# A transformer block's passage from attention to the MLP: fp32 copies of the first half, subtractions on VectorE, new places in memory

## The chip, the core and the metric

The kernel runs on one core of a Trainium2 chip. The time is device microseconds of one execution; the time before is the median of three runs. The profile is that of one further execution, and its span runs from the first to the last instruction. TensorE (PE, with its weight loads PEld), VectorE (DVE), ScalarE (ACT) and GpSimd (POOL) run side by side, SyncE (SP) issues most DMAs, and each engine takes its instructions in a fixed order.

## The reference

The block takes 1024 tokens of width 1024 through two attention branches and an MLP with squared ReLU. All is fp32. Cut to what the change touches:

```python
mixed = jnp.concatenate([rms_norm(oa, g_out_a[l]), rms_norm(ob, g_out_b[l])], axis=-1)
h_res = h_res + mixed @ w_out[l]
h = rms_norm(h_res, norm_mlp[l])
h_res = h_res + jnp.square(jax.nn.relu(h @ w_up[l])) @ w_down[l]
return rms_norm(h_res, norm_final)
```

Inside `ob`, three branches are gated and added: `out = gb0 * o_cmp + gb1 * o_sel + gb2 * o_win`.

## The kernel before, in words

**Precision.** Each fp32 operand of a large product is split in a high part (ScalarE copies it to fp32r) and a low part (VectorE or GpSimd subtracts the high part): `split`, lines 92 to 99, with lines 94, 95 for plain sources and 97, 98 for scaled ones from PSUM. A product is three matmuls: high by high, high by low, low by high.

**Attention.** The 8 token tiles of 128 rows are worked off in the order 5, 7, 6, 4, 3, 2, 1, 0. `b_done` (lines 851 to 860) ends a branch of a tile: it scales the output by its denominators and gates (line 857) and adds it to what was there (858), on GpSimd. Behind the second branch comes `finalize`. The output projection of a tile stands in `pieces`: one step transposes and splits the tile (700, 701), two steps multiply a column block each (709 to 711) and add it to the residual (713); the last also takes the row's norm (718 to 722) and scales the row by it (212, 214). After the last tile a few pieces are left, and the code of the transition pops them (line 1179).

**Transition.** The MLP's input must be transposed, scaled by the gain and split. Tiles 4 to 7 are the first half H0, tiles 0 to 3 the second, H1. A first-half step `h2_first(k)` transposes one block of 128 columns of four tiles into a PSUM bank of the kind T (there are two) and splits it into B11 (k below 4) or B21; the 8 steps are spread among the remaining pieces. The MLP's first product is made as a Strassen-Winograd scheme of 2 by 2 blocks with 7 products: 1, 2 and 3 take B11, B21, B22, and 4 to 7 take T4, T1, T2, T3, which are sums. `h2_second(j)` (lines 1154 to 1171) makes these for j from 0 to 3: with b the scaled blocks, T1 = b12 - b11, T2 = b22 - T1, T3 = b22 - b12, T4 = T2 - b21. As b11 and b21 exist only as split pairs, two subtractions take the place of one (1160 and 1161, 1167 and 1168). A ScalarE copy of b12 (1159) serves T3. GpSimd makes the first subtraction of T4 and the low parts of T3 and T1, VectorE those of T2 and T4. Product matmuls (`prod`, 1059 to 1065) of a j follow as soon as its blocks are there. The raw sums lie in two buffers under the tag dn, which the W_down blocks need afterwards.

**MLP loop.** For each of 16 groups g of 256 hidden columns, `up(g)` (1075 to 1111) makes the 7 products, adds them to four blocks c11, c21, c22, c12, and `c_done` squares them (1071), and splits them on ScalarE (1072) and GpSimd (1073). Group 0 is done in the transition. `down(g, t)` (1113 to 1127) multiplies them by W_down for 8 tiles, two column blocks each: a down group is 6 matmuls (1124 to 1126) into a bank of kind S and an addition to the residual on VectorE (1127). PSUM has in this stage 3 banks S, 2 T, 1 F and 2 O; a bank is given out in turn among its kind and must have been emptied. Products 1 and 6 are in T, 4 and 7 in O, 2 in F, 5 and 3 in S; 2 down groups follow in S's turn, and so on. Line 1095 empties product 2, 1106 and 1107 product 5, 1110 product 3. Each group's W_up and W_down blocks come by DMA from SP (1012, 1050) and are split (94, 95).

**Memory and order.** Pools are stacked from the left and from the right. When all attention pools on the right are closed, new ones begin at the right end, where cs2 was (gates, denominators), then vp (value tiles), wk and atp (softmax tiles, transposed ones), then the key tiles and the others. A new tile waits for the last readers of the old tiles that it lies over. Right pools of the MLP before: first h2p (all high parts B11 to T4, then all low ones), then mr (W_up blocks cA, cB, r2, r3 and split weights wa, wb). A list scheduler orders each engine's instructions at build time, by program order among those it takes to be ready; products can so be pulled ahead of their place. Product 2 of the next group often is.

Of the kernel before, what the change touches and what calls it, by code (L numbers as in the profile page):

```python
# [10 lines left out]
F32R = mybir.dt.float32r  # L11
BF = mybir.dt.bfloat16
FH = mybir.dt.float16
AF = mybir.ActivationFunctionType
# [42 lines left out]
def build(tc, A, out):  # L57
# [11 lines left out]
    def f32(ap):  # L69
        return ap.bitcast(F32)  # L70

    def mkpool(name, bufs=1, side="left", space=None):
        kw = dict(name=name, bufs=bufs, side=side, reuse_waits="tile")
        if space is not None:
            kw["space"] = space
            kw.pop("side")
        cm = tc.tile_pool(**kw)
        p = cm.__enter__()
        opened.append(cm)

        def close():
            opened.remove(cm)
            cm.__exit__(None, None, None)

        return p, close
# [6 lines left out]
    def split(hi, lo, src, scale=None, eng="A"):  # L92
        if scale is None:
            a = act.activation(hi, src, AF.Copy) if eng == "A" else dve.tensor_copy(hi, src)
            d = dve.tensor_sub(lo, src, f32(hi))  # L95
        else:
            a = act.activation(hi, src, AF.Copy, scale=scale)
            d = dve.scalar_tensor_tensor(lo, src, scale, f32(hi), op0=OP.mult, op1=OP.subtract)
        return a, d
# [247 lines left out]
    def bank(tag, shape, bufs=None):  # L347
        if tag == "F" and nbank[pst["second"]]["F"] == 0:
            tag = "O"
        n = nbank[pst["second"]][tag]  # L350
        p = pst["pool"] if tag in "OF" else psp
        t = p.tile([128, 512], F32, name=tag, tag=tag, bufs=n)
        if len(shape) == 3:
            return t[:, :shape[1] * shape[2]].rearrange("p (a b) -> p a b", a=shape[1])
        return t[:, :shape[1]]
# [495 lines left out]
    def b_done(i, br):  # L851
        o = OT[i, br]
        d = DEN[i, br] = cs2.tile([128, 8], F32, name="den", bufs=4)
        dve.tensor_scalar(d, o[:, :, 64], vsc[:, 2 + br:3 + br], None, op0=OP.mult)
        dve.reciprocal(d, d)
        pool.tensor_mul(d, d, gate[:, i].rearrange("p (h b) -> p b h", b=3)[:, 1 + br])
        pool.tensor_mul(o[:, :, 0:64], o[:, :, 0:64], d[:, :, None].to_broadcast([128, 8, 64]))
        pool.tensor_add(OC[i] if br else OB[i], o[:, :, 0:64], OC[i])
        if br == 0:
            finalize(i)  # L860

# [127 lines left out]

    cs2_close()  # L990
    NP = DFF // 256
    h2p, h2_close = mkpool("h2p", side="right")
    mr, mr_close = mkpool("mr", side="right")
    XN = ("B11", "B21", "B22", "T1", "T2", "T3", "T4")
    XH, XL = ({x: h2p.tile([128, 4, 512], F32R, name=x + y) for x in XN} for y in "hl")
    XOF = {1: "B11", 2: "B21", 3: "B22", 4: "T4", 5: "T1", 6: "T2", 7: "T3"}
    sso = cst.tile([128, NT, 4], F32, name="sso")
    e2 = cst.tile([128, NT], F32, name="e2")
# [6 lines left out]
    def small(tag, dt=F32, name=None):  # L1005
        p = mr if tag in ("cA", "cB", "r2", "r3") else ml[0]
        return p.tile([128, 512], dt, name=name or tag, tag=tag, bufs=1)

    def w_load(g, blk, tag):
        if g < NP:  # L1010
            t = RW[g, blk] = small(tag)
            sp.dma_start(t, A["w_up"][g, blk])

    def w_split(g, n, slot, src):
        if g < NP:
            t = (mr if slot in "ab" else ml[0]).tile([128, 2, 4, 128], F32R, name="w" + slot, tag="w" + slot, bufs=1)
            W[g, n] = t
            s = src.rearrange("p (k c) -> p k c", k=4)
            split(t[:, 0], t[:, 1], s)

    def w_prep(g, first=False):
        if g >= NP:
            return []
        A11, A12, A21, A22 = (RW[g, b] for b in range(4))

        def s1():
            if not first:
                w_split(g, 1, "a", A11)
            w_split(g, 4, "d" if first else "b", A22)

        def s2():
            dve.tensor_sub(A11, A11, A21)
            dve.tensor_add(A21, A21, A22)
            dve.tensor_sub(A22, A22, A11)
            w_split(g, 6, "c", A22)

        def s3():
            if not first:
                w_split(g, 2, "d", A12)
            dve.tensor_sub(A12, A12, A22)  # L1040

        def s4():
            w_split(g, 7, "e", A11)

        return [s1, s2, s3, s4]
# [13 lines left out]
    def prod(g, n, ps, ks=range(4)):  # L1059
        x, w = XOF[n], W[g, n]  # L1060
        for k in ks:
            xh, xl = XH[x][:, k], XL[x][:, k]
            pe.matmul(ps, w[:, 0, k], xh, start=k == 0, stop=False)  # L1063
            pe.matmul(ps, w[:, 0, k], xl, start=False, stop=False)  # L1064
            pe.matmul(ps, w[:, 1, k], xh, start=False, stop=k == 3)  # L1065
# [7 lines left out]
        pool.tensor_sub(lo, a, f32(hi))  # L1073

    def up(g):
        y = {n: bank(x, [128, 512], 2) for n, x in ((1, "T"), (4, "O"), (6, "T"), (2, "F"), (7, "O"), (5, "S"), (3, "S"))}
        for q in range(2):
            d_load(g, q)
        prod(g, 1, y[1])
        c11 = small("u0", name="c11")  # L1080
        act.activation(c11, y[1], AF.Copy)  # L1081
        w_split(g, 5, "a", RW[g, 2])
        for q in range(2):
            d_split(g, q)
        for q in range(2, 4):
            d_load(g, q)
        prod(g, 4, y[4])
        prod(g, 6, y[6])
        c12 = small("cA", name="c12")
        dve.tensor_add(c12, y[6], c11)  # L1090
        w_split(g, 3, "b", RW[g, 1])
        w_load(g + 1, 2, "r2")
        w_load(g + 1, 1, "r3")
        prod(g, 2, y[2])
        dve.tensor_add(c11, y[2], c11)
        c_done(g, 0, 0, c11)
        prod(g, 7, y[7])
        c22 = small("cB", name="c22")
        dve.tensor_add(c22, y[7], c12)
        c21 = small("u1", name="c21")  # L1100
        dve.scalar_tensor_tensor(c21, y[4], -1.0, c22, op0=OP.mult, op1=OP.add)
        c_done(g, 1, 0, c21)
        for q in range(2, 4):
            d_split(g, q)
        prod(g, 5, y[5])
        dve.tensor_add(c22, y[5], c22)
        dve.tensor_add(c12, y[5], c12)
        c_done(g, 1, 1, c22)
        prod(g, 3, y[3])
        dve.tensor_add(c12, y[3], c12)  # L1110
        c_done(g, 0, 1, c12)
# [34 lines left out]
    def h2_ps(h, k):  # L1146
        ps = transposes([hr(h * 4 + t)[:, k * 128:(k + 1) * 128] for t in range(4)])
        return ps.rearrange("p a b -> p (a b)")

    def h2_first(k):  # L1150
        x = "B11" if k < 4 else "B21"
        split(XH[x][:, k % 4], XL[x][:, k % 4], h2_ps(H0, k), scale=gm32[:, k:k + 1])

    def h2_second(j):
        raw = ml[0].tile([128, 4, 512], F32, name="wdx", tag="dn", bufs=2)
        T1, T2, T3, T4 = (raw[:, n] for n in range(4))
        ps = h2_ps(H1, j)
        g = gm32[:, j:j + 1]
        act.activation(T3, ps, AF.Copy, scale=g)
        dve.scalar_tensor_tensor(T1, ps, g, f32(XH["B11"][:, j]), op0=OP.mult, op1=OP.subtract)  # L1160
        dve.tensor_sub(T1, T1, f32(XL["B11"][:, j]))
        ps = h2_ps(H1, j + 4)
        g = gm32[:, j + 4:j + 5]
        dve.scalar_tensor_tensor(T2, ps, g, T1, op0=OP.mult, op1=OP.subtract)
        dve.scalar_tensor_tensor(T3, ps, g, T3, op0=OP.mult, op1=OP.subtract)
        split(XH["B22"][:, j], XL["B22"][:, j], ps, scale=g)
        pool.tensor_sub(T4, T2, f32(XH["B21"][:, j]))
        dve.tensor_sub(T4, T4, f32(XL["B21"][:, j]))
        for x, t, e in (("T2", T2, dve), ("T3", T3, pool), ("T4", T4, dve), ("T1", T1, pool)):
            act.activation(XH[x][:, j], t, AF.Copy)  # L1170
            e.tensor_sub(XL[x][:, j], t, f32(XH[x][:, j]))

    for blk, tag in enumerate(("cA", "r3", "r2", "cB")):
        w_load(0, blk, tag)
    w_split(0, 1, "a", RW[0, 0])
    w_split(0, 2, "b", RW[0, 1])
    rest = len(pieces)
    for n in range(rest):
        pieces.pop(0)[3]()
        for k in range(n * KD // rest, (n + 1) * KD // rest):  # L1180
            h2_first(k)
    wop_close()
    ml[0], ml_close = mkpool("mlq")
    y = {1: bank("F", [128, 512]), 2: bank("O", [128, 512]), 6: bank("O", [128, 512])}
    prod(0, 1, y[1])
    prod(0, 2, y[2])
    for f in w_prep(0, True):
        f()
    w_split(0, 5, "a", RW[0, 2])
# [12 lines left out]
    for j in range(5):  # L1202
        if j < 4:
            h2_second(j)
        if j:
            for n in (6, 7, 4) if j > 2 else (6, 7, 4, 3, 5):
                prod(0, n, y[n], ks=(j - 1,))
# [111 lines left out]
```

## Time and profile before

| | |
|---|---|
| median of 3 runs | 1414.26 us (1410.06 to 1418.48) |
| profiled execution | 1414.72 us, its span 1412.9 us, granted TensorE clock 0.98 |
| busy: PE, PEld | 1313.4 us (93%), 1110.6 us (79%) |
| busy: DVE, ACT, POOL | 970.4 (69%), 650.3 (46%), 512.0 us (36%) |

In a row of a timeline stand the start, the duration, the engine, the line of the kernel, the operation, the tile written and the one read, and in brackets how long the engine had been idle and what ended that. Neighbouring instructions of an engine overlap by a little, so the distance of two starts is the price of one in a row of many. A row of stages has for each engine the busy time and the number of instructions, in the order PE, PEld, DVE, ACT, POOL. A clock of 1.00 is 2.4 GHz.

### The profile page before, as it was taken

The numbers are of one execution on the slowest core, as the hardware profiler recorded it, in microseconds if no ns is written. First come the engines' busy times: TensorE is split into PE (matmuls) and PEld (weight loads), VectorE is DVE, ScalarE is ACT, GpSimd is POOL, SyncE is SP. The second block draws the span as 40 slices with busy tenths as digits, with TensorE's granted clock in tenths as the row PEclk, the third lists the DMA queues.
The fourth block names the chain that finished last, engine by engine and source line by source line (L and its number), as shares of the span: only waits on it lengthen the run. The fifth ranks groups of instructions, "written<-read, shape, count | busy, mean of one in ns | idle before, by whom it ended". The sixth has DMA issues, their size and how long they took to land.

```text
span 1412.9 us, 23742 instructions
## 1 busy us (share of the span) xinstructions
PE 1313.4 (93%) x8891; PEld 1110.6 (79%) x8891; DVE 970.4 (69%) x1953; ACT 650.3 (46%) x1212; POOL 512.0 (36%) x724
## 2 busy tenths in 40 slices
PE   7999999998987999899778999999999999999996
PEld 6788989888976777677656888888888888788885
DVE  6664565773458876878587667677767667776767
ACT  7462755872557866898553222222222212222216
POOL 3445473664445665577542110011111001111115
PEclk9999999999898999999999999999999999999998
DMA  6265382985538986686311121112111111111113
GB/s 189 68 113 120 87 185 51 206 184 145 93 107 180 172 152 129 143 157 96 82 30 34 56 59 46 45 46 60 45 60 46 59 41 50 55 50 61 45 46 134
DMA packets 265747, 131.68 MB, mean 93 GB/s; under 512 B 220064, under 2 KB 240544, under 8 KB 265632
## 3 DMA queue, kind: packets, MB, share of 16 engines
q1 hardware_dynamic: 265488, 129.90, 40.0%
q8 instruction: 70, 1.15, 0.3%
q14 instruction: 45, 0.37, 0.1%
q10 hardware_dynamic: 144, 0.26, 0.0%
HBM read 68.26 MB, written 8.39 MB: 54 GB/s over the span
## 4 chain that ended last, share of the span: by engine, by line
PE 57%; DVE 16%; DMA 8%; issue 7%; POOL 6%; ACT 5%; SPq 1%; DVEq 0%; POOLq 0%; ACTq 0%
PE S L1124 8%; PE S L1125 7%; PE S L1126 7%; PE F L335 3%; PE F L336 3%; PE F L337 3%; DMA u<-in_w_down_dram 3%; PE O L1064 2%; PE O L1063 2%; PE T L1065 2%; PE T L1063 2%; PE T L1064 2%; PE O L1065 2%; PE S L418 2%; DVE c L1071 1%
## 5 line engine op out<-in xcount | busy, mean ns | idle before, releaser
L1073 POOL TENSOR_TENSOR ul<-c,uh 128x512 fp32r<-128x512 f32 x64 | 92.5, 1454 | 557.8 <-ACT uh L1072 555.9
L1127 DVE SCALAR_TENSOR_TENSOR st<-S,r,st 128x512 f32<-128x512 f32 (+1 forms) x257 | 185.8, 742 | 70.3 <-PE S L1126 69.7
L1124 PE MATMUL S<-dn,uh 128*128 128x512 f32 (+1 forms) x514 | 203.2, 396 | 9.6 <-DVE c L1110 5.9
L1126 PE MATMUL S<-dn,ul 128*128 128x512 f32 (+1 forms) x514 | 200.6, 391 | 0.8 <-POOL ul L1073 0.8
L1125 PE MATMUL S<-dn,uh 128*128 128x512 f32 (+1 forms) x514 | 200.8, 391 | 0.0
L335 PE MATMUL F<-wh,hh 128*128 128x256 f32 (+1 forms) x576 | 167.2, 292 | 6.1 <-DVE st L214 3.2
L336 PE MATMUL F<-wl,hh 128*128 128x256 f32 (+1 forms) x576 | 166.5, 289 | 2.3 <-DVE wl L95 2.3
L337 PE MATMUL F<-wh,hl 128*128 128x256 f32 (+1 forms) x576 | 165.4, 288 | 0.0
L1124 PEld LDWEIGHTS S<-dn,uh 128*128 128x128 f32 x514 | 97.2, 189 | 37.8 <-DVE c L1110 12.2
L434 ACT ACTIVATE ns<-ns,mn 128x640 f32<-128x640 f32 (+7 forms) x152 | 110.7, 747 | 35.1 <-POOL mn L433 21.7
L335 PEld LDWEIGHTS F<-wh,hh 128*128 128x128 f32 x576 | 110.7, 193 | 8.2 <-DVE st L214 3.6
L450 POOL TENSOR_TENSOR hl<-ns,hl 128x640 f16<-128x640 f32 (+5 forms) x67 | 105.5, 1575 | 30.9 <-ACT hl L448 24.9
L1126 PEld LDWEIGHTS S<-dn,ul 128*128 128x128 f32 x514 | 97.0, 189 | 22.0 <-POOL ul L1073 1.5
L336 PEld LDWEIGHTS F<-wl,hh 128*128 128x128 f32 x576 | 111.3, 193 | 3.7 <-DVE wl L95 3.1
L1125 PEld LDWEIGHTS S<-dn,uh 128*128 128x128 f32 x514 | 97.4, 190 | 19.2
L337 PEld LDWEIGHTS F<-wh,hl 128*128 128x128 f32 x576 | 111.0, 193 | 0.5
L448 ACT ACTIVATE hl<-ns 128x640 f16<-128x640 f32 (+5 forms) x115 | 91.2, 802 | 5.8 <-DMA pt<-hl 5.0
L468 PE MATMUL O<-v,pt 128*128 128x65 f16 x694 | 77.3, 195 | 15.9 <-DMA pt<-hl 13.4
L1081 ACT ACTIVATE c<-T 128x512 f32<-128x512 f32 x15 | 9.0, 599 | 172.2 <-PE S L1125 172.2
L468 PEld LDWEIGHTS <-pt 128*128 128x128 f16 x694 | 63.9, 99 | 27.6 <-DMA pt<-hl 17.4
L418 PE MATMUL S<-kb,qb 128*128 128x384 f32 (+3 forms) x192 | 72.9, 385 | 12.6 <-DVE mn L429 8.9
L433 POOL TENSOR_SCALAR mn<-mn 128x1 f32<-128x1 f32 x130 | 43.7, 336 | 96.4 <-DVE mn L429 81.2
(372 smaller groups left out, 3625.1 us busy)
## 6 DMA issues: line engine op xcount, KB each, us to landing
u<-in_w_down_dram SPq DMA_DIRECT2D x64, 256.0 KB, 2.8
wr<-in_w_in_dram SPq DMA_DIRECT2D x44, 256.0 KB, 2.9
r<-in_w_up_dram SPq DMA_DIRECT2D x32, 256.0 KB, 2.7
st<-in_x_dram SPq DMA_DIRECT2D x8, 512.0 KB, 5.9
wor<-in_w_out_dram SPq DMA_DIRECT2D x16, 256.0 KB, 3.5
cA<-in_w_up_dram SPq DMA_DIRECT2D x16, 256.0 KB, 2.8
cB<-in_w_up_dram SPq DMA_DIRECT2D x16, 256.0 KB, 2.6
ns<-in_xT_dram SPq DMA_DIRECT2D x7, 512.0 KB, 5.1
```

The source lines that it names most:

```text
L335: pe.matmul(ps, hh[:, k, ts], hi, start=k == 0, stop=False)
L336: pe.matmul(ps, hh[:, k, ts], lo, start=False, stop=False)
L337: pe.matmul(ps, hl[:, k, ts], hi, start=False, stop=k == KD - 1)
L418: pe.matmul(ps[:, :w], u["q"], u["k"][:, cs], start=True, stop=False)
L434: u["exp"] = act.activation(ns[:, :n * 128], ns[:, :n * 128], AF.Exp, scale=-1.0, bias=mn[:, j:j + 1])
L450: pool.tensor_sub(lo, p, hi)
L468: pe.matmul(ps, ph, v[:, 64:129], start=t == 0, stop=False)
L1073: pool.tensor_sub(lo, a, f32(hi))
L1124: pe.matmul(ps, uh[:, ts], wd[:, 0, cs], start=j == 0, stop=False)
L1125: pe.matmul(ps, uh[:, ts], wd[:, 1, cs], start=False, stop=False)
L1126: pe.matmul(ps, ul[:, ts], wd[:, 0, cs], start=False, stop=j == 1)
L1127: dve.scalar_tensor_tensor(o[:, cs], ps, r2[:, t:t + 1], o[:, cs], op0=OP.mult, op1=OP.add)
```

## The change

In `b_done` the last two instructions go to VectorE for the last tile's second branch. The right side of memory is laid out anew: T4's high part first, then mr, then the other block tiles in pairs. In `up`, product 2 gets an S bank and product 3 the F bank. Four first-half steps come before the first weight splits and the remaining pieces, four stay among these. A second transposition of the first half, `h2_again(j)`, puts blocks j and j + 4 into fp32 tiles RB by ScalarE; they lie in the tiles v0 to v3, which the high and low parts of c11 and c21 use later. `h2_second` subtracts RB in place of split pairs; it has no GpSimd instruction and no ScalarE copy of b12 left.

```diff
@@ -854,8 +854,9 @@
         dve.tensor_scalar(d, o[:, :, 64], vsc[:, 2 + br:3 + br], None, op0=OP.mult)
         dve.reciprocal(d, d)
         pool.tensor_mul(d, d, gate[:, i].rearrange("p (h b) -> p b h", b=3)[:, 1 + br])
-        pool.tensor_mul(o[:, :, 0:64], o[:, :, 0:64], d[:, :, None].to_broadcast([128, 8, 64]))
-        pool.tensor_add(OC[i] if br else OB[i], o[:, :, 0:64], OC[i])
+        e = dve if i == ORD[-1] and br == 0 else pool
+        e.tensor_mul(o[:, :, 0:64], o[:, :, 0:64], d[:, :, None].to_broadcast([128, 8, 64]))
+        e.tensor_add(OC[i] if br else OB[i], o[:, :, 0:64], OC[i])
         if br == 0:
             finalize(i)
 
@@ -989,10 +990,15 @@
 
     cs2_close()
     NP = DFF // 256
+    XH, XL = {}, {}
+    h0p, h0_close = mkpool("h0p", side="right")
+    XH["T4"] = h0p.tile([128, 4, 512], F32R, name="T4h")
+    mr, mr_close = mkpool("mr", side="right")
     h2p, h2_close = mkpool("h2p", side="right")
-    mr, mr_close = mkpool("mr", side="right")
-    XN = ("B11", "B21", "B22", "T1", "T2", "T3", "T4")
-    XH, XL = ({x: h2p.tile([128, 4, 512], F32R, name=x + y) for x in XN} for y in "hl")
+    for x in ("B11", "B21", "B22", "T1", "T2", "T3", "T4"):
+        for y, X in (("h", XH), ("l", XL)):
+            if x not in X:
+                X[x] = h2p.tile([128, 4, 512], F32R, name=x + y)
     XOF = {1: "B11", 2: "B21", 3: "B22", 4: "T4", 5: "T1", 6: "T2", 7: "T3"}
     sso = cst.tile([128, NT, 4], F32, name="sso")
     e2 = cst.tile([128, NT], F32, name="e2")
@@ -1073,7 +1079,7 @@
         pool.tensor_sub(lo, a, f32(hi))
 
     def up(g):
-        y = {n: bank(x, [128, 512], 2) for n, x in ((1, "T"), (4, "O"), (6, "T"), (2, "F"), (7, "O"), (5, "S"), (3, "S"))}
+        y = {n: bank(x, [128, 512], 2) for n, x in ((1, "T"), (4, "O"), (6, "T"), (2, "S"), (7, "O"), (5, "S"), (3, "F"))}
         for q in range(2):
             d_load(g, q)
         prod(g, 1, y[1])
@@ -1151,39 +1157,45 @@
         x = "B11" if k < 4 else "B21"
         split(XH[x][:, k % 4], XL[x][:, k % 4], h2_ps(H0, k), scale=gm32[:, k:k + 1])
 
+    RB = {}
+
+    def h2_again(j):
+        for n, k in enumerate((j, j + 4)):
+            t = RB[k] = small("v%d" % (2 * (j % 2) + n), name="b%d1" % (n + 1))
+            act.activation(t, h2_ps(H0, k), AF.Copy, scale=gm32[:, k:k + 1])
+
     def h2_second(j):
         raw = ml[0].tile([128, 4, 512], F32, name="wdx", tag="dn", bufs=2)
         T1, T2, T3, T4 = (raw[:, n] for n in range(4))
         ps = h2_ps(H1, j)
-        g = gm32[:, j:j + 1]
-        act.activation(T3, ps, AF.Copy, scale=g)
-        dve.scalar_tensor_tensor(T1, ps, g, f32(XH["B11"][:, j]), op0=OP.mult, op1=OP.subtract)
-        dve.tensor_sub(T1, T1, f32(XL["B11"][:, j]))
+        dve.scalar_tensor_tensor(T1, ps, gm32[:, j:j + 1], RB[j], op0=OP.mult, op1=OP.subtract)
         ps = h2_ps(H1, j + 4)
         g = gm32[:, j + 4:j + 5]
         dve.scalar_tensor_tensor(T2, ps, g, T1, op0=OP.mult, op1=OP.subtract)
-        dve.scalar_tensor_tensor(T3, ps, g, T3, op0=OP.mult, op1=OP.subtract)
         split(XH["B22"][:, j], XL["B22"][:, j], ps, scale=g)
-        pool.tensor_sub(T4, T2, f32(XH["B21"][:, j]))
-        dve.tensor_sub(T4, T4, f32(XL["B21"][:, j]))
-        for x, t, e in (("T2", T2, dve), ("T3", T3, pool), ("T4", T4, dve), ("T1", T1, pool)):
-            act.activation(XH[x][:, j], t, AF.Copy)
-            e.tensor_sub(XL[x][:, j], t, f32(XH[x][:, j]))
+        dve.tensor_sub(T3, T2, RB[j])
+        dve.tensor_sub(T4, T2, RB[j + 4])
+        for x, t in (("T2", T2), ("T3", T3), ("T4", T4), ("T1", T1)):
+            split(XH[x][:, j], XL[x][:, j], t)
 
     for blk, tag in enumerate(("cA", "r3", "r2", "cB")):
         w_load(0, blk, tag)
+    rest = len(pieces)
+    for k in range(4):
+        h2_first(k)
     w_split(0, 1, "a", RW[0, 0])
     w_split(0, 2, "b", RW[0, 1])
-    rest = len(pieces)
     for n in range(rest):
         pieces.pop(0)[3]()
-        for k in range(n * KD // rest, (n + 1) * KD // rest):
+        for k in range(4 + n * 4 // rest, 4 + (n + 1) * 4 // rest):
             h2_first(k)
     wop_close()
     ml[0], ml_close = mkpool("mlq")
     y = {1: bank("F", [128, 512]), 2: bank("O", [128, 512]), 6: bank("O", [128, 512])}
     prod(0, 1, y[1])
     prod(0, 2, y[2])
+    for j in range(2):
+        h2_again(j)
     for f in w_prep(0, True):
         f()
     w_split(0, 5, "a", RW[0, 2])
@@ -1202,6 +1214,8 @@
     for j in range(5):
         if j < 4:
             h2_second(j)
+        if j < 2:
+            h2_again(j + 2)
         if j:
             for n in (6, 7, 4) if j > 2 else (6, 7, 4, 3, 5):
                 prod(0, n, y[n], ks=(j - 1,))
```

## Rows read from the trace of the kernel before

**Rows 1.** the slices of the span, TensorE.

```profile
PE   7999999998987999899778999999999999999996
```

**Rows 2.** stages: us, busy us (x) of each engine, clock, DMA share, GB/s.

```profile
690.50:698.30 7.80, 3.60 (x24) 2.64 (x24) 2.88 (x6) 2.88 (x9) 3.29 (x5) 1.00 0.50 151
698.30:718.30 20.00, 18.57 (x92) 14.73 (x92) 15.45 (x28) 13.06 (x25) 1.10 (x2) 0.91 0.14 41
718.30:749.70 31.40, 21.52 (x85) 13.75 (x85) 30.65 (x39) 16.15 (x27) 19.55 (x13) 0.95 0.05 18
```

**Rows 3.** timeline of GpSimd, last attention output: start us, us, what.

```profile
695.58 1.04 POOL L857 TENSOR_TENSOR ot<-ot,den 128x512 f32<-128x512 f32 x1
...
697.10 1.19 POOL L858 TENSOR_TENSOR ob<-ot,oc 128x512 f32<-128x512 f32 x1
```

**Rows 4.** timeline of TensorE from the last attention product to the second half.

```profile
693.89 0.20 PE L468 MATMUL O<-v,ptx 128*128 128x65 f16 x1
...
698.33 0.85 PE L360 MATMUL T<-c_ident,ob 128*128 128x128 f32 x4 [4.09 <-POOL ob L858]
...
700.89 1.05 PE L360 MATMUL T<-c_ident,st 128*128 128x128 f32 x4
...
708.23 1.03 PE L360 MATMUL T<-c_ident,st 128*128 128x128 f32 x8
```

**Rows 5.** timeline of VectorE, the second half's beginning.

```profile
718.30 0.74 DVE L1160 SCALAR_TENSOR_TENSOR wdx<-T,gm,B11h 128x512 f32<-128x512 f32 x1
...
719.56 0.69 DVE L95 TENSOR_TENSOR wb<-r,wb 128x512 fp32r<-128x512 f32 x1
720.16 0.68 DVE L1161 TENSOR_TENSOR wdx<-wdx,B11l 128x512 f32<-128x512 f32 x1
...
723.69 1.76 DVE L1161 TENSOR_TENSOR wdx<-wdx,B11l 128x512 f32<-128x512 f32 x1
```

**Rows 6.** instructions by line, 718.3 to 749.7: busy us, mean ns, idle before.

```profile
L1171 DVE TENSOR_TENSOR T2l<-wdx,T2h 128x512 fp32r<-128x512 f32 x4 | 5.1, 1266 | 0.0
...
L1168 DVE TENSOR_TENSOR wdx<-wdx,B21l 128x512 f32<-128x512 f32 x4 | 4.6, 1158 | 0.5 <-POOL wdx L1167 0.5
...
L1161 DVE TENSOR_TENSOR wdx<-wdx,B11l 128x512 f32<-128x512 f32 x4 | 3.8, 953 | 0.0
...
L1171 DVE TENSOR_TENSOR T4l<-wdx,T4h 128x512 fp32r<-128x512 f32 x4 | 3.8, 939 | 0.0
...
L1164 DVE SCALAR_TENSOR_TENSOR wdx<-T,gm,wdx 128x512 f32<-128x512 f32 x4 | 3.0, 744 | 0.1
...
L1170 ACT ACTIVATE T2h<-wdx 128x512 fp32r<-128x512 f32 x4 | 2.5, 631 | 0.9 <-DVE wdx L1164 0.9
```

**Rows 7.** timeline of GpSimd beside it.

```profile
723.18 1.72 POOL L1167 TENSOR_TENSOR wdx<-wdx,B21h 128x512 f32<-128x512 f32 x1
```

**Rows 8.** timeline of TensorE, the start of a later group's down products.

```profile
1044.26 0.39 PE L1063 MATMUL F<-B21h,wd 128*128 128x512 f32 x1
...
1046.76 0.39 PE L1124 MATMUL S<-dn,uh 128*128 128x512 f32 x1
...
1049.20 0.50 PE L1124 MATMUL S<-dn,uh 128*128 128x512 f32 x1 [0.47 <-DVE c L1110]
```

**Rows 9.** timeline of VectorE in the same stretch.

```profile
1042.33 0.69 DVE L95 TENSOR_TENSOR dn<-u,dn 128x512 fp32r<-128x512 f32 x1 [0.60 <-ACT dn L94]
...
1050.87 2.06 DVE L1127 SCALAR_TENSOR_TENSOR st<-S,r,st 128x512 f32<-128x512 f32 x3
```

**Rows 10.** the page's group of line 1124, then product 2 by tile B21h.

```profile
L1124 PE MATMUL S<-dn,uh 128*128 128x512 f32 (+1 forms) x514 | 203.2, 396 | 9.6 <-DVE c L1110 5.9
...
L1063 PE MATMUL F<-B21h,wd x60: 389/389/389, 757.4 to 1337.4; 128*128 128x512 f32 x60
```

**Rows 11.** stages: a middle iteration, the last one's start.

```profile
1005.00:1046.60 41.60, 41.23 (x182) 33.66 (x182) 28.98 (x43) 9.66 (x18) 5.28 (x4) 1.00 0.16 51
1371.00:1385.00 14.00, 11.89 (x43) 8.54 (x42) 12.48 (x18) 5.81 (x11) 4.72 (x4) 0.88 0.34 112
```

## The prediction, made before the changed kernel was run

> **What bounds the kernel now.** I read the slices of the span first: in slices 25 to 39 TensorE is at 9 tenths or more throughout [rows 1]. The loop over the 16 MLP groups is therefore bound by TensorE, and an edit there pays only where TensorE waits. Then I cut the transition into stages [rows 2]. From 690.5 to 698.3 no engine is busy for half of the time: the last attention outputs are awaited. From 698.3 to 718.3 TensorE shows 18.57 us of 20, in part with short transposes at a granted clock of 0.91. From 718.3 to 749.7 VectorE is busy for 30.65 of 31.4 us, while TensorE has only 85 matmuls. So the second half of the transposition is bound by VectorE, and what comes before it by a chain of several engines.
>
> **Part 1, the last attention output on VectorE.** GpSimd starts the multiplication at 695.58, does something else for half a microsecond, and ends the addition at 698.29; TensorE's wait of 4.09 us ends there [rows 3, 4]. That is 2.7 us. On VectorE I take 0.60 us an instruction, the distance between two neighbouring starts there (719.56 and 720.16) for two SBUF inputs [rows 5]. Two make 1.2 to 1.3 us, a gain of 1.4. No row shows this broadcast multiplication on VectorE; with 0.75 us each and one other instruction ahead the gain is 0.5, with nothing lost in between it is 1.5. What is late next is the output projection itself.
>
> **Part 2, four first-half steps earlier.** Each step is 4 transposes, one ScalarE copy, one VectorE subtraction of 0.75 us. Four of them now run among the last projection: four transposes that take 1.05 us, as long as eight do at 708.23, stand in its midst at 700.89 [rows 4]; the slow ones come right behind the wait. After the change they can run in the hole from 690.5 to 698.3, where VectorE is busy 2.88 of 7.8 us [rows 2]. Their tiles no longer lie over the gate table and denominators that the last output reads, but over softmax tiles, read last by the transposing DMAs. Without that cover they would cost VectorE 4 x 0.66 = 2.6 us again. On the path I count 1 us for the transposes and 2.6 us of VectorE time until 718.3.
>
> Against that stand 16 new transposes for the fp32 second copy, placed before the second half: 8 of them take 1.03 us [rows 4], so 2 us on TensorE, with four ScalarE copies behind two PSUM buffers 2.6 us. The second half's VectorE work begins at 718.30 now [rows 5]. TensorE has to finish the projection first, at 708.2 less 1.4 and 1.0, then the transposes of the last two steps (1.0), the 24 matmuls of products 1 and 2 (5.5 at 0.227 us), those 16 (2.6) and the first four of the second half (0.6, a little over half of 1.03): 715.5. **Parts 1 and 2 together: -2.8 us**, bounds -5 (the new transposes find holes) and -0.5 (they are wholly in the way). The four weight loads on SP now lie over the value tiles, which the last attention product reads at about 694 [rows 4]. Nothing is queued behind them on SP but the first W_down loads, which their tiles hold back until the projection is done, and the splits that use them stand behind that projection too: nothing, and 1 us where TensorE would come to product 1 sooner.
>
> **Part 3, the loop over the second half.** Before, one of four rounds has 8 VectorE instructions, 4 of SBUF alone (0.60 us from start to start [rows 5]) and 4 that read PSUM (744 ns where those show 0.68 [rows 5, 6], so 0.66): 20.2 us for 32. Their groups are longer than that: the T2 subtraction means 1266 ns, the one of line 1168 1158, lines 1161 and T4 953 and 939, against about 690 unstretched [rows 5, 6]. Summed, (0.58 + 0.47 + 0.26 + 0.25) x 4 = 6.2 us of stretch. The stretched ones stand beside GpSimd: 1.76 us for line 1161 at 723.69 while GpSimd subtracts from 723.18 to 724.90, and 0.68 with GpSimd quiet at 720.16 [rows 5, 7]. The PSUM-reading ones do not stretch (744 ns) [rows 6].
>
> After, a round has 9 VectorE instructions, 3 of PSUM and 6 of SBUF: 5.58 us, 22.3 for four. The six others of the stage (weight splits and sums, 3.7 us) stay. GpSimd has no subtraction left but the one of the first finished block, which now waits until the copies in its tile are read: I leave 1 us for it. Every result now goes ScalarE then VectorE, seven ScalarE instructions a round at 0.63 us or less [rows 6], 4.4 of 5.58: enough, with some holes; 1.5 us instead of 0.75. Sum 22.3 + 3.7 + 1.0 + 1.5 = 28.5 against 31.4: **-2.9 us**. Bounds: -4.7 (no holes, no stretch) and +1 (ScalarE becomes the order-giver). The stage behind it, to 757.4, just moves.
>
> A rule speaks against this part. The Trainium skill, Perfetto Trace Analysis, Optimizing Scalar/DVE Operations, says that where VectorE is saturated, giving work to ScalarE or even GpSimd may make sense, though GpSimd shares a read port and may not help. Read by its first half, four more instructions on the saturated engine cost 22.3 - 20.2 = 2.1 us, and the sum would be higher by 5 (1407); by its second half the trace's stretch agrees with me.
>
> **Part 4, the bank swap, fifteen times.** In the loop product 3 now sits in the ring of three S banks that the down groups use. The third down group waits for line 1110 to empty it: 0.47 us of idleness, and 0.6 us of lost issue with the slow first matmul [rows 8]; over the loop 5.9 us of waits [rows 10], about 9 in all. After, that bank holds product 5, emptied earlier. But the fourth group needs the bank of the first, and VectorE, in one unbroken row, empties this from 1050.87 to 1051.6 [rows 9]; TensorE, from 1046.76 with 19 matmuls of 0.227 us, would want it at 1051.1. So between 0 and 0.6 us an iteration is gained. VectorE has a hole of 0.60 us in that row, waiting for a weight copy [rows 9], which the changed order may fill; I take 0.35 x 14 = **-4.9 us**, bounds -9 and +2.
>
> Product 2 was until now pulled ahead of its iteration: its 12 matmuls fill the time between product 3 and the first down group (the F matmuls from 1044.26, down from 1046.76) [rows 8], all 15 times (60 matmuls of its first kind, the first at 757.4 and the last at 1337.4, a whole iteration before the end) [rows 10]. In the S ring it must wait for a late down group of the iteration before. Then it fills the same hole in its own iteration; the sum of matmuls is unchanged, but the last iteration, where nothing is left to pull ahead, gets its filler: now TensorE is busy 11.89 us of 14 there at a granted clock of 0.88, against 41.23 of 41.6 at 1.00 in an iteration of the middle [rows 11]. I take 2.7 us gained there and 0.7 lost at 757: **-2.0 us**, bounds 0 and -3.8.
>
> **The sum.** -2.8 - 2.9 - 4.9 - 2.0 = -12.6. The profiled execution took 1414.72 us (span 1412.9 and 1.8 around it), 0.5 above the median of the runs. 1414.7 - 12.6 = 1402.1, **1402 us**.
>
> **The rivals.** (a) VectorE's row takes the place of the bank: the wait moves from the third to the fourth down group, Part 4 gives 0 and 1 us at the end. For it: that row has no room before 1050.87. Against it: the hole in it. 1414.7 - 2.8 - 2.9 - 1.0 = 1408.0 us. Chance 0.20.
>
> (b) Slower: the filler is lost. If product 2 runs before the last down groups, the hole before the next down groups keeps only products 5 and 3: 24 matmuls of 0.227 us, 5.4 us, where now 36 fill it, 8.2 us. 2.7 us an iteration, 1402 + 38 = 1440, or a part of it; it decides from the point where more than one product's matmuls leave the hole. Against it: TensorE has other products (6, 7) that fill the earlier holes, and the S ring holds product 2 back. Chance 0.08.
>
> (c) More instructions on VectorE simply cost more, the stretch not being GpSimd's: Part 3 gives 22.3 + 6.2 + 3.7 + 0.75 = 33.0 instead of 28.5, 1406.6 us. The groups of rows 6 speak against it, since only instructions with two SBUF inputs stretch. Chance 0.09. It is what the first half of the Trainium skill's sentence would give.
>
> (d) The early steps do not come early, because a softmax tile is freed only when the last transposing DMA lands, just before the last attention product near 694 [rows 4], and both PSUM buffers are then held: Parts 1 and 2 give -1.4 and the time is 1403.5. Chance 0.08.
>
> **The numbers.** My forecast gets 0.55. About 0.5% (7 us) is what a measurement of this kernel can tell from no change; its three runs lie between 1410.06 and 1418.48. So faster begins below 1407.2: nearly all of the forecast (0.51), 0.08 of (a), half of (c), most of (d): 0.70. Slower, above 1421.4, is (b) nearly alone: 0.07; 0.23 remains. The range goes down to 1393 (bounds of Parts 3 and 4 together) and up to 1412, past (a) and (c) with the weak ends of Parts 1 and 2.
>
> **What would show it.** The first second-half subtraction at about 715.5 instead of 718.3; no GpSimd subtraction but line 1073's and no SBUF subtraction over 1.3 us until the end of that loop, which takes some 28.5 us; no down matmul waiting for line 1110; product 2 in S within its own iteration, and a last iteration in which TensorE's clock stays at 1.00. I am wrong if the fourth down group waits on line 1127 in every iteration, if TensorE stands still before the first down group, or if ScalarE is what the subtractions of the second half wait for.

## The result, and the profile after

The change made the kernel slower: 1431.03 us median of four runs (1429.92 to 1432.00) beside 1416.37 us for the kernel before on the same chip, ratio 1.0108, 95% interval 1.0068 to 1.0148. The profiled span is 1430.1 us against 1412.9. The forecast of 1402 us and its range of 1393 to 1412 were wrong, and wrong in sign.

To see where the 17.2 us lie, both spans are cut at five events that each trace has: the last matmul of line 470 (the last attention product), the first second-half subtraction, the last low part of the second half, and the first addition of a down group (line 1127 before, 1133 after).

| stretch | before | after | difference |
|---|---|---|---|
| start to the last attention product | 694.05 | 690.39 | -3.66 |
| from there to the second half | 24.25 | 28.84 | +4.59 |
| loop over the second half | 31.35 | 25.90 | -5.45 |
| from there to the first down addition | 7.75 | 10.91 | +3.16 |
| the rest, the MLP loop | 655.50 | 674.06 | +18.56 |

The first line is no effect. Six programs of this study that are the same up to there (before, e2, e4, e5, e9, e10) give 690.6 to 696.0 in their profiles, with nothing changed in that part. So stretches are compared, not spans. The transition as a whole lost 2.3 us, and the MLP loop 18.6.

**The MLP loop.** First TensorE and then VectorE in one iteration of after, by the timelines; it answers to [rows 8, 9].

```profile
1258.25 0.39 PE L1069 MATMUL S<-B21h,wd 128*128 128x512 f32 x1
...
1261.19 0.39 PE L1071 MATMUL O<-T3h,we 128*128 128x512 f32 x1
1261.42 0.39 PE L1069 MATMUL S<-T1h,wa 128*128 128x512 f32 x1
...
1266.86 0.39 PE L1130 MATMUL S<-dn,uh 128*128 128x512 f32 x1
...
1272.07 0.50 PE L1130 MATMUL S<-dn,uh 128*128 128x512 f32 x1 [0.90 <-DVE st L1133]
```

```profile
1255.96 0.69 DVE L1096 TENSOR_TENSOR c<-T,c 128x512 f32<-128x512 f32 x1 [0.62 <-ACT c L1087]
...
1259.84 1.35 DVE L95 TENSOR_TENSOR dn<-u,dn 128x512 fp32r<-128x512 f32 x2 [2.52 <-ACT dn L94]
1261.17 0.69 DVE L1101 TENSOR_TENSOR c<-S,c 128x512 f32<-128x512 f32 x1
1261.78 0.68 DVE L1105 TENSOR_TENSOR c<-O,c 128x512 f32<-128x512 f32 x1
...
1271.27 2.06 DVE L1133 SCALAR_TENSOR_TENSOR st<-S,r,st 128x512 f32<-128x512 f32 x3
```

Product 2 (B21h, now into S) stands **ahead of the last two matmuls of product 7** (T3). Behind product 7 only products 5 and 3 are left here before the first down group: 24 matmuls, 5.67 us from 1261.19 to 1266.86. Two rows of before that stand beside [rows 8, 9], TensorE's last matmul of product 7 and VectorE's sum of it:

```profile
1038.60 0.39 PE L1065 MATMUL O<-T3h,we 128*128 128x512 f32 x1
```

```profile
1040.45 0.68 DVE L1099 TENSOR_TENSOR c<-O,c 128x512 f32<-128x512 f32 x1
```

There the first down matmul came at 1046.76 [rows 8], 8.16 us and about 36 matmuls later: products 5, 3, and nearly all of the next iteration's product 2. Product 7's sum (line 1099, after 1105) opens VectorE's row of sums, squares and splits that the down groups wait for. That row takes 9.49 us after, from 1261.78 to 1271.27; before it took 10.42, from 1040.45 to 1050.87 [rows 9]. So the cover shrank by 2.49 us and the row by 0.93. The row also begins sooner behind product 7's last matmul, by 0.59 us instead of 1.85, so that in this iteration, one of the mildest, TensorE waits 0.90 us for line 1133 where it waited 0.47 for line 1110 before [rows 8]. Over the whole span the page's group of the first down matmul has 23.0 us of idleness where [rows 10] have 9.6:

```profile
L1130 PE MATMUL S<-dn,uh 128*128 128x512 f32 (+1 forms) x514 | 203.7, 399 | 23.0 <-DVE st L1133 12.1
```

In the built program of before, products 7, 5, 3 and the next iteration's product 2 follow each other in this way in every iteration but the last, which has no next one. In after the order changes from one iteration to the next. In nine of the 15 product 2 lies ahead of the last one or two matmuls of product 7, as above, and 24 matmuls cover the row. In the other six it lies behind product 7, as here:

```profile
1129.77 0.39 PE L1071 MATMUL O<-T3h,we 128*128 128x512 f32 x1
1129.99 0.39 PE L1069 MATMUL S<-B21h,wd 128*128 128x512 f32 x1
...
1138.97 0.50 PE L1130 MATMUL S<-dn,uh 128*128 128x512 f32 x1 [0.66 <-ACT uh L1078]
```

There 36 matmuls stand behind product 7, but 12 of them are the product 2 whose sum and square the row must still make, and the first down matmul waits for ScalarE's copy of that square. TensorE stands still for 0.8 to 2.2 us at the down groups of the nine, and for 0.7 to 2.2 us at those of the six. What the distances of TensorE's matmul starts have beyond 0.227 us, summed from 758 us on where it is over 0.12 us, is 12.5 us before and 27.6 after: 15.1 of the 18.6.

**The transition.** TensorE behind the last attention product:

```profile
690.39 0.19 PE L470 MATMUL O<-v,ptx 128*128 128x65 f16 x1
696.70 2.37 PE L360 MATMUL T<-c_ident,st 128*128 128x128 f32 x8 [6.12 <-DVE B11l L98]
699.38 1.12 PE L360 MATMUL T<-c_ident,ob 128*128 128x128 f32 x4 [0.30 <-DVE B11l L98]
```

VectorE at that time:

```profile
693.43 0.68 DVE L859 TENSOR_TENSOR ob<-ot,oc 128x512 f32<-128x512 f32 x1
694.04 0.68 DVE L95 TENSOR_TENSOR wa<-cA,wa 128x512 fp32r<-128x512 f32 x1
...
695.91 0.74 DVE L98 SCALAR_TENSOR_TENSOR B11l<-T,gm,B11h 128x512 fp32r<-128x512 f32 x1
```

The last attention output is ready at 694.1, but its transposes begin at 699.38. In TensorE's order two early first-half steps (the 8 transposes at 696.70) stand ahead of them; these wait for a T bank, and the bank is held by the first early step, whose ScalarE copy comes at 694.84 and whose subtraction at 695.91, both behind the two weight splits. The stages of the second half and behind it, columns as in [rows 2]:

```profile
719.20:745.20 26.00, 23.04 (x103) 14.56 (x103) 24.15 (x38) 15.62 (x27) 1.29 (x1) 1.00 0.07 21
745.20:756.00 10.80, 7.69 (x20) 5.08 (x20) 9.19 (x13) 4.08 (x7) 3.02 (x3) 0.68 0.08 24
```

VectorE's 38 instructions take 24.15 us where 39 took 30.65 [rows 2]. The stretch of [rows 6] is nearly gone:

```profile
L95 DVE TENSOR_TENSOR T2l<-wdx,T2h 128x512 fp32r<-128x512 f32 x4 | 3.3, 824 | 0.0
...
L1176 DVE TENSOR_TENSOR wdx<-wdx,b 128x512 f32<-128x512 f32 x4 | 2.7, 685 | 0.0
```

In the stage behind it TensorE's granted clock falls to 0.68 of full speed, and ScalarE waits for W_down:

```profile
745.26 1.15 ACT L94 ACTIVATE dn<-u 128x512 fp32r<-128x512 f32 x2 [2.54 <-DMA u<-in_w_down_dram]
...
750.40 0.63 ACT L94 ACTIVATE dn<-u 128x512 fp32r<-128x512 f32 x1 [3.47 <-DMA u<-in_w_down_dram]
750.94 0.61 ACT L1078 ACTIVATE uh<-c 128x512 fp32r<-128x512 f32 x1
```

### The profile page after: what moved, and what is told of

Read it like the earlier page. It is cut to its first block, busy times and chain, and to the rows that moved or that the text cites. A ratio compares the mean times of both kernels' runs of the same rounds, so it can differ in the third digit from the quotient of the medians.

```text
span 1430.1 us, 23798 instructions
## 1 busy us (share of the span) xinstructions
PE 1326.1 (93%) x8923; PEld 1116.0 (78%) x8923; DVE 977.0 (68%) x1959; ACT 652.6 (46%) x1216; POOL 492.6 (34%) x710
## 4 chain that ended last, share of the span: by engine, by line
PE 54%; DVE 15%; DMA 11%; issue 7%; POOL 7%; ACT 6%; SPq 1%; POOLq 0%; DVEq 0%; ACTq 0%
PE S L1130 7%; PE S L1131 7%; PE S L1132 6%; DMA u<-in_w_down_dram 5%; PE F L336 3%; PE F L335 3%; PE F L337 3%; DVE c L1077 2%; PE T L1070 2%; PE T L1069 2%; PE T L1071 2%; PE T L360 2%; PE S L418 2%; DVE dn L95 2%; PE O L1069 1%
## 5 line engine op out<-in xcount | busy, mean ns | idle before, releaser
L1079 POOL TENSOR_TENSOR ul<-c,uh 128x512 fp32r<-128x512 f32 x64 | 89.3, 1403 | 600.7 <-ACT uh L1078 505.3
L1132 PE MATMUL S<-dn,ul 128*128 128x512 f32 (+1 forms) x514 | 194.4, 390 | 1.2 <-POOL ul L1079 1.1
L94 ACT ACTIVATE dn<-u 128x512 fp32r<-128x512 f32 x64 | 40.2, 630 | 90.9 <-DMA u<-in_w_down_dram 82.2
```

Source lines behind the costliest of these rows:

```text
L1132: pe.matmul(ps, ul[:, ts], wd[:, 0, cs], start=False, stop=j == 1)
```

## The experiments

Ratios are to the kernel before on the same chip, with 95% intervals. Stretches are those of the table above.

### The bank swap alone, and all but it

e1 is after with the old banks in the loop; e2 is before with the new ones.

```diff
-(2, "S"), (7, "O"), (5, "S"), (3, "F")
+(2, "F"), (7, "O"), (5, "S"), (3, "S")
```

> The changed kernel with the old banks in the loop (product 2 in F, product 3 in S). Theory A (the bank swap is the loss, 18.6 us between the first addition of a down group and the end of the span; the transition gained 1.4): 1431.0 - 18.6 = 1412.5 us, 0.995 to 1.000 of the kernel before, and the matmul order 7, 5, 3, 2 before the first down group is back in every iteration. Rival B (the loop is slow because the new tiles of the transition moved its buffers, or because of the state the transition leaves): still 1425 to 1432 us.

> The kernel before with the bank swap alone. Theory A: 1416.4 + 18.6 = 1435 us, 1.013 of before, and TensorE waits for line 1127 (a bank emptied late) in most iterations. Rival B: 1414 to 1418 us, 1.00.

e1: 1416.07 us, 1.0008 (0.9984 to 1.0031), MLP loop 655.13. e2: 1435.71 us, 1.0137 (1.0098 to 1.0177), MLP loop 674.21. The swap is the whole loss of the loop, and the other parts together change nothing that can be measured.

### Product 2 written behind product 7

e4 is e2 with product 2, its sum and its square written behind product 7 and its sums.

```diff
-        prod(g, 2, y[2])
-        dve.tensor_add(c11, y[2], c11)
-        c_done(g, 0, 0, c11)
         prod(g, 7, y[7])
...
         c_done(g, 1, 0, c21)
+        prod(g, 2, y[2])
+        dve.tensor_add(c11, y[2], c11)
+        c_done(g, 0, 0, c11)
```

> As e2_swap_alone, with product 2 and its sum written behind product 7, c22 and c21 in the program. Theory E (in the swap product 2 runs before the last matmuls of product 7, so c22 and c21 come 3 to 4 us later, VectorE's row ends later, and the first down bank is emptied late): product 7 is now complete first, and two thirds or more of e2's loss goes, 1416 to 1422 us. Rival F (the loss is that product 2 is tied to the S ring and can no longer fill the time before the first down group, whatever the order): 1430 to 1436 us.

1427.21 us, 1.0069 (1.0037 to 1.0100), MLP loop 667.91: 6.3 of the 18.7 us come back. Timelines of TensorE, then VectorE:

```profile
1171.56 0.39 PE L1065 MATMUL O<-T3h,we 128*128 128x512 f32 x1
...
1180.21 0.50 PE L1124 MATMUL S<-dn,uh 128*128 128x512 f32 x1
...
1185.62 0.50 PE L1124 MATMUL S<-dn,uh 128*128 128x512 f32 x1 [0.80 <-DVE st L1127]
```

```profile
1172.59 0.68 DVE L1096 TENSOR_TENSOR c<-O,c 128x512 f32<-128x512 f32 x1
...
1176.83 0.68 DVE L1101 TENSOR_TENSOR c<-S,c 128x512 f32<-128x512 f32 x1
1177.43 1.46 DVE L95 TENSOR_TENSOR wd<-r,wd 128x512 fp32r<-128x512 f32 x1
1178.82 0.68 DVE L1071 SCALAR_TENSOR_TENSOR c<-c 128x512 f32<-128x512 f32 x1
...
1184.83 2.06 DVE L1127 SCALAR_TENSOR_TENSOR st<-S,r,st 128x512 f32<-128x512 f32 x3
```

The cover is back, 8.65 us from product 7's last matmul to the first down matmul. But product 2's sum and the split that waits for its matmuls now lie inside VectorE's row, which takes 12.24 us (1172.59 to 1184.83) instead of 10.42. So the order of writing is part of the cause only, and neither expectation held: theory E wanted two thirds of the loss back, rival F nothing.

### Product 2 in another bank, and two ways to lose the cover

e9 and e10 are before with banks changed, `(2, "T") … (3, "F")` and `(2, "F") … (3, "F")`.

> The kernel before with product 2 in the T ring and product 3 in the F bank (before: 2 in F, 3 in S). Product 2 is then bound to its own iteration, as after the change, but to a bank that comes free early, and the S ring loses a tenant instead of changing one. Its order of matmuls is the same in every iteration: product 7 whole, product 5, a quarter of product 3, product 2, the rest of product 3, and then the down groups. Theory R (what costs 18.7 us is the S ring: product 2 waits for a late down group there, and the order changes from iteration to iteration): the loop behind the transition takes 655 to 657 us and the time is 1414 to 1418 us. Theory O (what costs it is that product 2 no longer runs an iteration ahead, so that its sum and its square stand in VectorE's row ahead of the first down groups): the loop takes 668 to 674 us, 1427 to 1434 us, and TensorE waits for line 1127 by 0.8 us or more at the start of every down group row.

> The kernel before with product 3 in the F bank beside product 2 (S keeps product 5 and the down groups). Product 2 still runs an iteration ahead, but only behind 13 matmuls of the down groups, so it no longer fills the time between product 3 and the first down group. Theory O (own iteration): nothing of product 2 stands in VectorE's row of its iteration, the loop takes 655 to 658 us, 1414 to 1419 us. The filler theory (rival b of the prediction): TensorE has 24 matmuls instead of 36 ahead of the first down group, stands still there by up to 2.7 us an iteration, and the loop takes 670 to 696 us, 1430 to 1455 us. Theory R (S ring) says as theory O here, since product 2 is not in S.

e9: 1461.71 us, 1.0332 (1.0307 to 1.0358), MLP loop 700.67. e10: 1436.96 us, 1.0150 (1.0112 to 1.0187), MLP loop 674.16. Theories R and O fell: theory R wanted 655 to 657 for e9, theory O 668 to 674 for e9 and 655 to 658 for e10. The filler theory, 670 to 696 for e10, held. TensorE at the start of the down groups, e9 and then e10:

```profile
1066.99 0.50 PE L1124 MATMUL S<-dn,uh 128*128 128x512 f32 x1 [3.27 <-ACT uh L1072]
```

```profile
1051.84 0.39 PE L1065 MATMUL F<-B22h,wb 128*128 128x512 f32 x1
1052.07 0.39 PE L1124 MATMUL S<-dn,uh 128*128 128x512 f32 x1
1052.29 0.39 PE L1125 MATMUL S<-dn,uh 128*128 128x512 f32 x1
1053.18 0.50 PE L1126 MATMUL S<-dn,ul 128*128 128x512 f32 x1 [0.50 <-POOL ul L1073]
1054.39 0.51 PE L1124 MATMUL S<-dn,uh 128*128 128x512 f32 x1 [0.71 <-ACT uh L1072]
```

In e10 product 2 of the next iteration comes behind 13 of the down matmuls instead of ahead of them: it still runs ahead of its iteration, and S has lost a tenant, not changed one. The loop loses 18.7 us, as much as in after, by two gaps in nearly every iteration, both waits for what ScalarE and GpSimd make of VectorE's squares. This is the prediction's rival (b), the lost filler, by itself. In e9, 36 matmuls stand behind product 7, but only 6 of them come behind product 2, so its sum (at 1064.33 on VectorE), its square and its copy come last, and TensorE waits 3.27 us for them.

| version | product 2 | matmuls from product 7 to the first down group | MLP loop |
|---|---|---|---|
| before | an iteration ahead | 36 | 655.5 |
| e10 | an iteration ahead | 24 | 674.2 |
| after, e2 | own, in nine iterations ahead of product 7's end, in six behind it | 24, 36 | 674.1, 674.2 |
| e4 | own, right behind product 7 | 36 | 667.9 |
| e9 | own, late | 36 | 700.7 |

What holds all five together: TensorE must have matmuls between product 7 and the first down group that cover VectorE's row, **and these must not be matmuls whose result that row needs**. Of the orders in this table only the one with the next iteration's product 2 there has such a filler. The S ring is not needed to explain the loss, since e10 has it without; it is how product 2 was made to leave its place.

### The wait on product 3's bank

e5 is before with product 3 in a T bank (2 stays in F); e6 is e3, below, with the same.

> The kernel before with product 3 in a T bank instead of S; product 2 keeps F, and the matmul order of the loop stays 7, 5, 3, 2 before the first down group. No down group can wait for line 1110 any more. Theory G (VectorE's unbroken row is the next thing, the fourth down group waits for line 1127 instead): the loop keeps 654 to 656 us from the first addition to the end, 0.999 to 1.001 of before. Rival H (the wait on line 1110 was a true loss of 0.6 us an iteration): the loop is 5 to 9 us shorter, 0.994 to 0.997.

> As e3_late_first with product 3 in a T bank. By theory G the same as e3, 1412 to 1416 us; by rival H 5 to 9 us under it, 1406 to 1410.

e5: 1414.79 us, 0.9997 (0.9974 to 1.0020), MLP loop 655.64. e6: 1417.30 us, 0.9997 (0.9973 to 1.0022), 656.19. The wait for line 1110 [rows 8, 10] is gone, and nothing is gained. e5's page has in its place:

```profile
L1124 PE MATMUL S<-dn,uh 128*128 128x512 f32 (+1 forms) x514 | 200.7, 396 | 8.4 <-DVE st L1127 4.6
```

That is rival (a): the wait moves on to the fourth down group, at nearly the same price.

### Early steps and second copies

e3 is e1 with the eight first-half steps spread as before, none early; e8 has two early; e7 is e3 with one second copy ahead of the second half and the others a round ahead each.

```diff
-    for k in range(4):
-        h2_first(k)
...
-        for k in range(4 + n * 4 // rest, 4 + (n + 1) * 4 // rest):
+        for k in range(n * KD // rest, (n + 1) * KD // rest):
```

> As e1_banks_back, with the eight first-half steps spread among the remaining pieces as before (none early); the fp32 copies, the new memory places and the VectorE output stay. Theory C (the early steps stand ahead of the last tile's transposes in TensorE's fixed order; it was idle 6.12 us for them and the second half began 4.3 us later against the last attention product): 4 to 6 us under e1, about 1408 us, 0.993 to 0.996 of before. Rival D (the second half begins late because of the 16 new transposes and copies): no more than 1 us from e1, 1411.5 to 1413.5.

> As e1_banks_back with two early first-half steps instead of four. Theory C (steps three and four stand ahead of the last tile's transposes on TensorE, and two steps hold both PSUM buffers): the last tile is transposed in front of further steps, 1.5 to 3.5 us earlier than in e1 against the last attention product (8.99 us there, 4.28 before), and the second half begins at 26 to 27.5 us instead of 28.8. If it stays at 28 or more, what delays is not the number of early steps.

> As e3_late_first, but of the fp32 copies only the first round's stand ahead of the second half, the others each one round ahead of their use. In e3 the second half begins 26.36 us after the last attention product, against 24.25 before, in spite of the output moved to VectorE. Rival D (the 16 new transposes and their copies delay the second half): it begins 1 to 2 us earlier, about 25 us, and the loop over the second half stays at 26 us. Otherwise (the delay is the new order of the projection and the splits): 26 to 27 us.

| version | median, ratio (95%) | to the second half | second half | to the first down addition |
|---|---|---|---|---|
| before | | 24.25 | 31.35 | 7.75 |
| e1, four early | 1416.07, 1.0008 (0.9984 to 1.0031) | 28.79 | 25.90 | 10.99 |
| e8, two early | 1420.99, 1.0036 (1.0016 to 1.0055) | 26.48 | 27.53 | 11.17 |
| e3, none early | 1415.43, 0.9983 (0.9953 to 1.0014) | 26.36 | 25.89 | 11.25 |
| e7, copies later | 1417.45, 1.0005 (0.9982 to 1.0029) | 25.77 | 26.45 | 11.25 |

Without early steps the last output's transposes begin 3.96 us behind the last attention product instead of 8.99, and the second half 2.4 us sooner, not the 4 to 6 of theory C. It is still 2.1 us later than before. TensorE keeps the times of before up to the point where the second half's first transposes begin there, 22.55 us behind the last attention product; in e3 the new transposes begin at 22.61. The row of before and those of e3:

```profile
716.60 0.60 PE L360 MATMUL T<-c_ident,st 128*128 128x128 f32 x4
```

```profile
713.04 0.60 PE L360 MATMUL T<-c_ident,st 128*128 128x128 f32 x4
...
713.94 1.13 PE L360 MATMUL T<-c_ident,st 128*128 128x128 f32 x8
...
715.51 1.24 PE L360 MATMUL T<-c_ident,st 128*128 128x128 f32 x8 [0.44 <-ACT b L1165]
```

In e3 20 transposes end at 716.75, just ahead of the second half at 716.79: the 16 new ones, with ScalarE's copies (line 1165) in between, and the second half's first four. So the 2.1 us are these transposes and copies. e7, which lets eight of them wait, moves half a microsecond into the loop and gains nothing. In e8 the last output's transposes begin 6.31 us behind the last attention product, behind a wait of 6.12 us for a bank that the first of two early steps holds; the second half begins no later than in e3 even so. Of the ratios only e8's is clear of 1. Most of that loss is in the MLP loop, 659.2 us in the profiled execution: its order of matmuls differs from one iteration to the next there, though only first-half steps were moved. What e1, e3 and e7 gain and lose shows in the stretches alone.

### The W_down pieces of the first group

e11 is e3 with the third and fourth W_down pieces loaded into tiles that come free sooner, and two of the splits placed in the last round.

```diff
+        if j == 3:
+            d_load(0, 2, "cB")
+            d_split(0, 0)
+            d_load(0, 3, "u2")
+            d_split(0, 2)
```

> e3 (the change without the bank swap and without early first-half steps) with the first group's third and fourth W_down pieces loaded into tiles that are free earlier, and the splits of the first and the third moved ahead of the last round's end. In e3 the time from the end of the second half to the first down addition was 11.25 us against 7.75 before, ScalarE standing still for 2.64 and 3.55 us there until these pieces had landed. If that wait is what gives back the gain of the second half, the stage falls to 8 or 9 us with the loop over the second half at 25.9 to 27, and the time is 2 to 3 us below e3: ratio to before 0.996 to 0.998. If VectorE's own row sets the stage (14 instructions of 0.6 us and 0.7, about 9 us, of which only 1 us is idle), it stays at 10 to 11 us, and the time is that of e3, 0.998 to 1.000.

1413.50 us of twelve runs, 0.9992 (0.9973 to 1.0010). The stage to the first down addition falls from 11.25 to 8.60 us, with the second half at 26.49: the wait for these pieces was what gave the gain back. Its ScalarE now waits for VectorE there, not for a DMA:

```profile
745.14 1.15 ACT L94 ACTIVATE dn<-u 128x512 fp32r<-128x512 f32 x2 [2.85 <-DVE T4l L95]
...
749.54 0.63 ACT L1078 ACTIVATE uh<-c 128x512 fp32r<-128x512 f32 x1 [2.73 <-DVE c L1077]
```

The three stretches sum to 61.80 us against 63.35 before and 65.65 after. 1.5 us of 1416 is below what these runs can tell from nothing, so no version was shown to beat the kernel before.

## Why the prediction was wrong

**Part 4, the bank swap (-4.9 and -2.0; measured +18.6).** The step that failed is "Then it fills the same hole in its own iteration; the sum of matmuls is unchanged". The hole is not filled by any matmuls. Those of its own iteration either come before product 7 ends, and leave the hole (after), or are themselves awaited by the row that the hole is waiting for (six iterations of after; e4, e9). I had the right rival, (b), and priced it at 38 us from 12 matmuls an iteration; 18.6 us were lost, half of that and the "part of it". The row that began sooner and took 0.93 us less gave some of the cover back; what else did is not shown. Its threshold was wrong as well: it was said to decide where more than one product leaves the hole, and e10 shows that one product does it. The argument held against it, that the S ring holds product 2 back, did not help: so held back, product 2 still comes ahead of product 7's end in nine iterations, and in the other six it feeds the row.

The -4.9 was worth 0 by itself: e5 takes that wait away without the swap and gains nothing, as rival (a) said. I weighed "VectorE, in one unbroken row" correctly and then let a hole of 0.60 us in it count as room. The term for the last iteration came true in its number by luck. TensorE loses 4.6 us there before (1378 to 1385) and 1.9 after (at 1397.0 and 1401.3), 2.7 gained, as I took. But no filler was gained: before and after, 24 matmuls and 5.67 us lie in that iteration between product 7's last matmul and the first down matmul. Half of the gain is the clock, which stays at 1.00 where [rows 11] show 0.88; before, it was at 0.51, near the lower level of 1.2 GHz, from 1382.5 to 1384.8, behind four gaps of TensorE, and after there are two gaps. Why there are fewer gaps is not shown. The gain is inside the +18.6. The stage of after, columns as in [rows 11]:

```profile
1388.00:1402.00 14.00, 12.38 (x53) 9.44 (x52) 11.17 (x17) 5.51 (x11) 5.18 (x4) 1.00 0.32 106
```

**Parts 1 and 2 (-2.8; measured +4.6).** The step that failed is "After the change they can run in the hole". The engines had room; the two T banks and the order of ScalarE and VectorE, which evict them, did not. Rival (d) saw the banks held, from a later release, and took a lost gain for the worst case; that TensorE's order puts early steps ahead of the transposes on the path was in no part. e3 against e1 prices it at 2.4 us. The new transposes and copies cost 2.1 in e3, near the 2.6 of the forecast, but nothing was gained to pay for them. The attention output on VectorE brought its transposes forward by 0.3 (4.28 to 3.96), not 1.4, and nothing of that is left at the next transposes of first-half steps, at 10.14 before and 10.25 in e3. Its two instructions take 0.68 us each as estimated, but line 214 and a wait for GpSimd's line 722 stand between them.

**Part 3 (-2.9; measured -5.45, of which 3.2 given back).** The mechanism was right: GpSimd quiet, no stretch. The GpSimd subtraction that stayed cost one instruction, 1.26 us at 737.13. The Trainium skill, Perfetto Trace Analysis, Optimizing Scalar/DVE Operations, says that GpSimd shares a read port with VectorE, so that moving work between the two might not help. The trace agrees: T2's subtraction fell from 1266 to 824 ns mean. The other half, that giving work away may make sense where VectorE is saturated, did not hold here, and rival (c) fell. Two terms were mis-sized. Of the "six others", put at 3.7 us, two instructions of 0.68 us were left in the loop; the rest had gone to the stage behind it. That stage did not "just move": it grew by 3.16 us, and the W_down pieces were late there (e11). Both stages together went from 39.10 to 36.81 us, -2.3, close to the forecast for a reason that it did not name.

So the predicted sum of -12.6 met, from the last attention product on, +4.6 - 2.3 + 18.6 = +20.9, and 3.7 of that was hidden in the profiled executions by the varying time ahead of it.

## What to carry to other kernels

Before moving a product or a bank, ask of every matmul in a hole whose result it makes: a filler from the next iteration covers a chain, one from the same iteration may be a link of it. In e5 a wait that ended on a bank was worth nothing: it is worth its length only if the engine that empties the next bank is not already in one unbroken row. And a step placed early by its engine's idle time must also find its banks free and not stand ahead of what is on the path.

## What was not expected

The order of matmuls that the built program has depends on when banks come free, so that a change of two bank names made an even loop into one that differs from iteration to iteration, and so did e8's move of first-half steps ahead of the loop. How a loop so changed would run with its order held fixed in S was tried only by e4's way of writing it. The clock of TensorE fell to 0.68 in the stage behind the second half, where it had 0.78 before, each a mean of the two levels, while TensorE had 20 matmuls in 10.8 us.
